# A batched matmul with scale and add: which two tiles GpSimd's queue stores, and in which groups of partitions

## The chip, the cores and the metric

One core of a Trainium2 chip. The metric is the device time of one execution in microseconds; lower is better.

## The reference

```python
batch, m, k, n = 16, 512, 1024, 768
x:         (batch, m, k) float32
weight:    (k, n)        float32
scale:     0.1
add_value: (batch, m, n) float32

def reference(x, weight, scale, add_value):
    return (scale * np.matmul(x, weight) + add_value).astype(np.float32)
```

## The kernel before

The 16 batches are taken as one matrix of 8192 rows, that is 64 tiles of 128 rows. The rows are dealt out so that partition p of a group of 16 tiles holds 16 neighbouring rows of the output: `x_v`, `add_v` and `out_v` are views with the axes partition, group, tile, column. A transfer of n tiles of one group therefore moves n x 3072 B in one piece per partition for `add_value` and `out`, and n x 4096 B for `x`.

The buffers are fixed tensors, and the kernel says by hand who waits for what. `xs` holds 16 tiles of `x` (in four "moves" of 4 tiles), `ao` holds 32 tiles: `add_value` is loaded into a slot, the result is written over it, and it is stored from there; tile t has slot t % 32, so tile t + 32 can only be loaded when tile t is stored. At the start the last slots of `ao` hold the weight.

Each engine has one job:

- SP (SyncE) issues the transfers in the order of the list `STREAM` (lines 22 to 29), all on one queue. An entry is a kind, a first tile and a number of tiles: "w" weight, "x" a load into `xs`, "a" a load of `add_value` into `ao`, "o" a store from `ao`, and "a+" a bookkeeping step with no transfer. Ahead of each entry SP waits for what it needs (`need`): an "x" for the casts that free the slots (line 116), an "a" for the earlier loads and for the stores that free its slots (lines 120 to 132), an "o" for an earlier store and for DVE's results (line 142).
- ACT (ScalarE) and GpSimd run `mover` (line 150): they cast `x` from `xs` to bfloat16 in `va`, 8 instructions each for a move, in strips of 32 partitions, laid out for the transpose.
- DVE (VectorE) casts the weight, transposes the moves into `xt` (line 178), and finishes pairs of tiles: scale times the product, plus `add_value`, into `ao` (line 187). `made` counts finished tiles.
- PE (TensorE) runs `product` (line 207): 8 weight loads and 16 matmuls per tile.

GpSimd has a second job, around which the change turns. After its first two rounds of casts (`TURN_AT = 2`, that is tiles 0 to 31) it waits until the tiles of `PAIR` are finished and stores these two tiles itself, on its own DMA queue, in three transfers that share the 128 partitions as `BY_POOL` says (lines 246 to 248). Then it goes on with its casts. SP leaves these two tiles out of its own stores, and waits for GpSimd's stores (`aside_sem`) ahead of the load that overwrites the first of the two slots:

```python
                if s <= PAIR.start + A_SLOTS <= last:
                    need(aside_sem, 16 * len(BY_POOL))
```

Before, `PAIR` is tiles 8 and 15, and the load in question is that of `add_value` for tiles 40 to 47.

Of the kernel before, what the change touches and what calls it, by code (L numbers as in the profile page):

```python
# [10 lines left out]
R = 16  # L11
X_SLOTS = 16
A_SLOTS = 32
# [8 lines left out]
STREAM = [  # L22
# [6 lines left out]
]  # L29
FIRST, ENDING = (0, 8), 48  # L30
PAIR, TURN_AT = slice(8, 16, 7), 2
BY_POOL = [(122, 6), (0, 98), (98, 24)]


@with_exitstack
def kernel(
# [23 lines left out]
    out_v = out_f.rearrange("(g p t) n -> p g t n", p=P, t=R)  # L60
# [10 lines left out]
    ao = const.tile([P, A_SLOTS, N], fp32, name="ao")  # L71
# [10 lines left out]
    aside_sem = tc.alloc_semaphore("aside")  # L82
# [8 lines left out]
        return t % A_SLOTS  # L91

    def store_pair(eng, p, n):
        assert PAIR.stop <= R and PAIR.stop <= A_SLOTS
        eng.dma_start(out_v[p:p + n, 0, PAIR, :], ao[p:p + n, PAIR, :]).then_inc(aside_sem, 16)  # L95

    def sync_engine(eng):
        groups, stores, known = 0, [], {}

        def need(sem, value):  # L100
            if known.get(sem, 0) < value:
                eng.wait_ge(sem, value)  # L102
                known[sem] = value

        for at, (op, s, n) in enumerate(STREAM):
# [14 lines left out]
            elif op == "a":  # L120
# [4 lines left out]
                if s <= PAIR.start + A_SLOTS <= last:  # L125
                    need(aside_sem, 16 * len(BY_POOL))
                if s >= A_SLOTS:
# [109 lines left out]
    s, n = FIRST  # L237
# [4 lines left out]
    with tc.tile_critical(no_gpsimd_drain=True):  # L242
        sync_engine(nc.sync)
        mover(nc.scalar, nc.scalar.copy, 0, by_act)
        mover(nc.gpsimd, nc.gpsimd.tensor_copy, 1, by_pool, pool_go, 0, TURN_AT)
        nc.gpsimd.wait_ge(made, MADE + PAIR.stop)
        for p, n in BY_POOL:
            store_pair(nc.gpsimd, p, n)
        nc.gpsimd.addr_align(HALF_BLOCK, offset=PAST, max_nops=0)
        mover(nc.gpsimd, nc.gpsimd.tensor_copy, 1, by_pool, pool_go, TURN_AT, T // X_SLOTS - TURN_AT)  # L250
        vector_engine(nc.vector)
        tensor_engine(nc.tensor)
# [40 lines left out]
```

## Time and profile before

| | |
|---|---|
| median of 3 runs | 207.06 us (207.04 to 207.12) |
| the profiled execution | 206.85 us, its span 205.5 us |
| bytes moved | 87.04 MB, of these 61.87 MB read from and 25.17 MB written to HBM |
| busy PE | 167.5 us (82%) |
| busy POOL, ACT, DVE | 137.4, 134.7, 98.0 us |
| SP's queue, GpSimd's queue | 86.25 MB, 0.79 MB |

The span runs from the first to the last instruction of the profiled execution. The queue named hardware_dynamic is SP's, the one named software_dynamic is GpSimd's. All transfers of both are carried out by the same 16 DMA engines. In the timelines a row gives start, duration, engine, line and operation, and in brackets the idle time ahead of it with what ended it.

### The profile page before, as it was taken

The page shows a single profiled execution, that of the slowest core. Times are in us where ns is not written, and L with a number is a line of the kernel's source. Part 1 is how long each engine was busy: PE and PEld are TensorE (multiplying, and loading weights), DVE is VectorE, ACT ScalarE, POOL GpSimd, SP SyncE. Part 2 cuts the span into 40 slices and gives each one's busy share as a digit, 9 for nine tenths or more (in the row PEclk, how much of TensorE's full clock was granted, in tenths as well). Part 3 has the DMA queues.
Part 4 walks back from the last instruction along what each step waited for, and adds up shares of the span by engine and source line. Part 5 has one row for each costly group of instructions (what it writes and reads, how often), then busy time and mean ns, then how long its engine had stood idle before and what let it go on. Part 6 is the DMA issues. An engine that isn't in the chain of part 4 may idle for free.

```text
span 205.5 us, 2223 instructions
## 1 busy us (share of the span) xinstructions
PE 167.5 (82%) x1008; PEld 50.4 (25%) x512; DVE 98.0 (48%) x66; ACT 134.7 (66%) x129; POOL 137.4 (67%) x135
## 2 busy tenths in 40 slices
PE   0000099999999999999999999999999997999900
PEld 0000022233322333223332233332333322333200
DVE  0004525537555555465555555555552853455330
ACT  2049980699999906999999059999991099920000
POOL 0049994699999916999999549999992099930000
PEclk9999999999999999999999999999999999999995
DMA  8989999999999899999999999999999999998997
GB/s 287 427 372 438 440 485 408 392 437 459 446 459 459 357 459 408 408 426 413 455 404 450 431 416 464 434 411 421 440 431 415 437 448 421 493 459 364 423 440 304
DMA packets 4065, 87.04 MB, mean 424 GB/s; under 512 B 480, under 2 KB 480, under 8 KB 1120
## 3 DMA queue, kind: packets, MB, share of 16 engines
q1 hardware_dynamic: 3856, 86.25, 98.1%
q0 software_dynamic: 208, 0.79, 0.9%
q14 instruction: 1, 0.01, 0.0%
HBM read 61.87 MB, written 25.17 MB: 424 GB/s over the span
## 4 chain that ended last, share of the span: by engine, by line
DMA 38%; PE 36%; POOL 10%; ACT 5%; issue 4%; DVE 3%; SPq 1%; POOLq 0%; DVEq 0%; ACTq 0%
PE mm L210 36%; DMA out_dram<-ao 22%; DMA xs<-in_x_dram 15%; POOL va L163 9%; ACT va L163 5%; DVE xt L178 2%; DVE ao L187 1%; POOL out_dram L95 1%; SPq L130 0%; SPq L118 0%; DVEq L176 0%; SPq L102 0%; POOLq L156 0%; POOLq L158 0%; POOLq L153 0%
## 5 line engine op out<-in xcount | busy, mean ns | idle before, releaser
L210 PE MATMUL mm<-w_bf,xt 128*128 128x256 bf16 (+1 forms) x1008 | 167.5, 327 | 28.0 <-DVE xt L178 27.1
L163 POOL CAST va<-xs 32x1024 bf16<-32x1024 f32 x128 | 135.2, 1056 | 44.2 <-DMA xs<-in_x_dram 36.8
L163 ACT CAST va<-xs 32x1024 bf16<-32x1024 f32 x128 | 133.4, 1042 | 45.2 <-DMA xs<-in_x_dram 42.2
L187 DVE SCALAR_TENSOR_TENSOR ao<-mm,ao 128x1536 f32 (+1 forms) x32 | 56.2, 1756 | 72.9 <-PE mm L210 68.9
L208 PEld LDWEIGHTS <-xt 128*128 128x128 bf16 x512 | 50.4, 98 | 144.6 <-issue 116.6
L178 DVE STREAM_TRANSPOSE xt<-va 128x1024 f32<-128x1024 f32 x32 | 39.4, 1234 | 8.4 <-POOL va L163 6.3
L171 DVE CAST w_bf<-ao 128x3072 bf16<-128x3072 f32 x2 | 4.5, 2240 | 18.1 <-DMA ao<-in_weight_dram 18.1
L152 ACT ACT_TABLE_LOAD x1 | 1.3, 1283 | 1.3 <-SPq L242 1.3
L95 POOL DMA_DIRECT2D out_dram<-ao x3 | 2.0, 672 | 0.0
L274 POOL MEMSET const-float32-0.0<- 128x1 f32 x1 | 0.1, 98 | 0.2 <-issue 0.2
L274 POOL MEMSET const-bfloat16-1.0<- 128x1 bf16 x1 | 0.1, 101 | 0.0
L274 POOL MEMSET const-float32-1.0<- 128x1 f32 x1 | 0.1, 98 | 0.0
L274 POOL MEMSET const-uint8-127<- 128x1 uint8 x1 | 0.1, 98 | 0.0
## 6 DMA issues: line engine op xcount, KB each, us to landing
xs<-in_x_dram SPq DMA_DIRECT2D x7, 4096.0 KB, 20.9
ao<-in_add_value_dram SPq DMA_DIRECT2D x6, 3072.0 KB, 15.7
out_dram<-ao SPq DMA_DIRECT2D x3, 3072.0 KB, 27.4
ao<-in_add_value_dram SPq DMA_DIRECT2D x1, 6144.0 KB, 24.2
out_dram<-ao SPq DMA_DIRECT2D x1, 6144.0 KB, 31.2
out_dram<-ao SPq DMA_DIRECT2D x1, 4608.0 KB, 14.9
xs<-in_x_dram SPq DMA_DIRECT2D x2, 2048.0 KB, 21.0
ao<-in_weight_dram SPq DMA_DIRECT2D x2, 1536.0 KB, 16.8
```

Of the source, the lines that this page charges most:

```text
L95: eng.dma_start(out_v[p:p + n, 0, PAIR, :], ao[p:p + n, PAIR, :]).then_inc(aside_sem, 16)
L152: eng.preload_act_table(mybir.ActivationFunctionType.Copy)
L163: copy(va[q % VA_BUFS][32 * b:32 * b + 32, :, a, :], src[32 * a:32 * a + 32, :, b, :]).then_inc(count, 1)
L171: eng.tensor_copy(w_bf[:, s:s + n, :], ao[:, W_AT + s:W_AT + s + n, :]).then_inc(casts, n)
L178: eng.transpose(xt[:, 2 * half:2 * half + 2, :, :].rearrange("p i c m -> p (i c m)"), va[move % VA_BUFS][:, q:q + 2 * KC, :, :].bitcast(fp ...
L187: eng.scalar_tensor_tensor(a, mm[:, q:q + 2, 0:N], float(scale), a, op0=mybir.AluOpType.mult, op1=mybir.AluOpType.add).then_inc(made, 2)
L208: eng.ldweights(x_j, tile_position=(0, 0))
L210: m = eng.add_instruction(mybir.InstMatmult(start_tensor_calc=(j == 0), stop_tensor_calc=(j == KJ - 1), tile_size=(P, P), tile_position=(0 ...
L274: nc = _bacc.Bacc("TRN2", target_bir_lowering=False, num_devices=1)
```

## The change

GpSimd stores tiles 16 and 23 where it stored 8 and 15. SP stores 8 to 15 whole, and 17 to 22 in place of 16 to 23. GpSimd's three transfers take 5, 48 and 75 partitions in place of 6, 98 and 24. The wait for them moves with the pair: it now stands ahead of the load of `add_value` for tiles 48 to 55. `store_pair` computes the group of the pair, since tiles 16 to 23 lie in the second group of 16.

```diff
@@ -22,14 +22,14 @@
 STREAM = [
     ("w", 0, 4), ("w", 4, 4), ("a", 0, 8),
     ("x", 8, 8), ("a", 8, 8), ("x", 16, 8), ("a", 16, 16), ("x", 24, 8),
-    ("x", 32, 8), ("a+", 16, 16), ("o", 0, 8), ("o", 9, 6), ("a", 32, 8), ("x", 40, 8),
-    ("a", 40, 8), ("x", 48, 8), ("o", 16, 8), ("o", 24, 8), ("a", 48, 8), ("x", 56, 4),
+    ("x", 32, 8), ("a+", 16, 16), ("o", 0, 8), ("o", 8, 8), ("a", 32, 8), ("x", 40, 8),
+    ("a", 40, 8), ("x", 48, 8), ("o", 17, 6), ("o", 24, 8), ("a", 48, 8), ("x", 56, 4),
     ("x", 60, 4), ("a", 56, 8), ("o", 32, 16), ("o", 48, 12),
     ("o", 60, 4),
 ]
 FIRST, ENDING = (0, 8), 48
-PAIR, TURN_AT = slice(8, 16, 7), 2
-BY_POOL = [(122, 6), (0, 98), (98, 24)]
+PAIR, TURN_AT = slice(16, 24, 7), 2
+BY_POOL = [(123, 5), (0, 48), (48, 75)]
@@ -91,8 +91,9 @@
     def store_pair(eng, p, n):
-        assert PAIR.stop <= R and PAIR.stop <= A_SLOTS
-        eng.dma_start(out_v[p:p + n, 0, PAIR, :], ao[p:p + n, PAIR, :]).then_inc(aside_sem, 16)
+        assert PAIR.start // R == (PAIR.stop - 1) // R and PAIR.stop <= A_SLOTS
+        at = slice(PAIR.start % R, (PAIR.stop - 1) % R + 1, PAIR.step)
+        eng.dma_start(out_v[p:p + n, PAIR.start // R, at, :], ao[p:p + n, PAIR, :]).then_inc(aside_sem, 16)
```

## The prediction

> **What bounds the kernel now.** I read the page first: the span, the DMA line of the 40 slices, and the queues.
>
> ```profile
> span 205.5 us, 2223 instructions
> DMA  8989999999999899999999999999999999998997
> DMA packets 4065, 87.04 MB, mean 424 GB/s; under 512 B 480, under 2 KB 480, under 8 KB 1120
> q1 hardware_dynamic: 3856, 86.25, 98.1%
> q0 software_dynamic: 208, 0.79, 0.9%
> ```
>
> The packets of SP's queue (q1) fill 98.1% of the time of 16 engines, those of GpSimd's queue (q0) 0.9%. Nothing is left to fill: 87.04 MB at 424 GB/s is the 205.3 us. No engine of arithmetic is near that; the table by stretches shows it, and that TensorE runs at the full granted clock until its work ends at 197.4.
>
> ```profile
> core 0: us, PE busy (x) PEld busy (x) DVE busy (x) ACT busy (x) POOL busy (x), PEclk, DMA share, GB/s
> 82.00:123.00 41.00, 40.79 (x250) 12.33 (x126) 22.76 (x16) 32.53 (x32) 34.20 (x36) 1.00 1.00 425
> 164.00:197.40 33.40, 30.18 (x183) 8.99 (x92) 17.23 (x12) 16.68 (x16) 16.55 (x16) 1.00 1.02 440
> 197.40:205.50 8.10, 0.00 (x0) 0.00 (x0) 0.00 (x0) 0.00 (x0) 0.00 (x0) 0.66 0.78 335
> ```
>
> PE is at 40.79 of 41 us too, but after its end come 8.1 us in which only the DMA engines work off their backlog. So the end is that of the last DMA engine, and what matters is which one that is.
>
> The views do not number the engines, but the trace's packet records give queue, size, start and duration, and a packet starts 3 or 4 ns before the previous one of its engine ends. Following this, all records fall into 16 chains, each with the same 216 data packets of q1. None has an idle time worth naming (two of 0.16 and 0.31 us). The chains, ordered by end; "6/98/24" are the packets that GpSimd's three stores put on the chain, "stores" is how much longer its store packets took than the usual one of their size:
>
> ```
> chain   6/98/24  sum  stores us  end us
> Y       1/0/2     3    0.00      204.28
> G1      1/7/0     8    0.01      204.65
> G2      1/7/0     8    0.00      204.68
> G3      1/7/0     8    0.00      204.88
> ten     0/7/2     9    0.00-0.01 204.93 to 205.42
> G4      1/7/0     8    0.20      205.37
> X       1/0/2     3    1.60      205.50
> ```
>
> This is the finding on which the forecast rests. One engine, X, is slow in every store: its 912 ns packets take 23 to 69 ns more, its 1815 ns ones 33 to 71 more, 1.60 us in all; no other has more than 0.20. X ends last although it has only 3 packets of GpSimd's, not 8 or 9. One of these packets (6144 B, two tiles of a partition) takes 0.234 us, which agrees with q0's row: 0.9% of 16 times 205.5 is 29.6 us, by 128 is 0.23. With 8, X would end at 206.67. So the split of GpSimd's stores holds X back from deciding the end, and the changed numbers are the split.
>
> **The split after.** The sets in the table show how GpSimd's queue deals partitions out: 6, 14 and 12 engines are the largest numbers up to 16 that divide 6, 98 and 24, and each transfer starts where the one before stopped: the second's 14 leave out just X and Y, the third's 12 leave out just the four G, and the first's six are these six. In ring order: four G, then X and Y (which of the two is first the trace does not say), then ten others. The Trainium skill, in DMA: Bandwidth & Descriptors, section "Why a DMA increments its semaphore by 16 and not by 1", states the same: the largest count that divides the slowest dimension, on consecutive engines from a round-robin cursor.
>
> By the same sets, 5 partitions go on 5 engines (the four G and the first of the pair), 48 on all 16 with 3 each, 75 on 15 with 5 each, starting at the second of the pair and going round to the last G. That makes 9 on each G, 4 on the first of the pair, 8 on the second and on the ten. Only one engine is relieved, not two. If X is the first: 4 for 3, X ends 0.23 later, at 205.74; G4 at 205.61, Y (+5) at 205.45, the ten 0.23 earlier. If X is the second: 8 for 3, 5 x 0.234 = 1.17 later, at 206.67.
>
> There is a third way. Before, the ring is moved on by 6 + 14 + 12 = 32, two whole turns, so every execution starts at the same engine whether or not the place is kept from one execution to the next. After it is 5 + 16 + 15 = 36: if the place is kept, each execution starts four engines on, and X has 8 or 9 packets in at least three of four. A weak sign for that: in the first load of the trace the chains start in the order X 2.247, ..., G 2.268, ..., Y 2.287, up to G 2.518, 2.627 and 2.888. Three G are the last three of 16, as if they were the last engines of the ring and X and Y close to its head; then the first transfer did not begin at the head, though it is the first of the execution.
>
> **The other edits, each at its place.** SP's order of instructions stays; two sizes change places.
>
> ```profile
> out_dram<-ao SPq DMA_DIRECT2D x1, 2304.0 KB, 28.2
> 73.13 0.82 SPq L143 DMA_DIRECT2D out_dram<-ao  x2
> 96.02 0.34 SPq L130 DMA_DIRECT2D ao<-in_add_value_dram  x1
> 96.47 0.84 SPq L118 DMA_DIRECT2D xs<-in_x_dram  x1
> ```
>
> Tiles 8 to 15 whole: 0.79 MB more in SP's queue from 73, at 424 GB/s 1.86 us per engine, ahead of add-value 32 to 39 (issued 96.02) and x 40 to 47 (96.47). Tiles 17 to 22 for 16 to 23 give the same back from 117. From there the bytes queued are as before, so add-value 48 and x 56, 60 land when they did. Sum at the end: 0. Between, x 40 lands 1.86 later, and this is what waits for it:
>
> ```profile
> 120.68 34.96 POOL L163 CAST va<-xs 32x1024 bf16<-32x1024 f32 x32 [4.95 <-DMA xs<-in_x_dram]
> 129.51 1.25 DVE L178 STREAM_TRANSPOSE xt<-va 128x1024 f32<-128x1024 f32 x1 [1.05 <-POOL va L163]
> 131.91 1.76 DVE L187 SCALAR_TENSOR_TENSOR ao<-mm,ao 128x1536 f32 x1 [1.15 <-PE mm L210]
> 174.49 1.69 PE L210 MATMUL mm<-w_bf,xt 128*128 128x512 bf16 x9 [1.13 <-DVE xt L178]
> ```
>
> GpSimd's casts start at 122.5, the transpose at 131.4, ending 132.6. PE ends tile 39 just ahead of the 131.91 row, so it stalls some 0.7 us ahead of tile 40. Before tile 56 it waits 1.13 us for data that comes no later than now: the 0.7 goes into that. Uncovered, it would push the last issue from 197.41 to 198.1, and the engines reach that store's packets only from 200.6 on (the earliest chain), X at 201.8.
>
> ```profile
> 197.41 0.33 SPq L143 DMA_DIRECT2D out_dram<-ao  x1
> ```
>
> So 0, and 0.7 as its upper bound. The wait for GpSimd's stores:
>
> ```profile
> 95.25 1.04 POOL va L163
> 96.28 1.36 POOL out_dram L95 x2
> 97.65 18.69 DMA out_dram<-ao
> ...
> 116.40 0.33 SPq L130
> 116.82 0.39 SPq L118
> 117.32 27.42 DMA out_dram<-ao
> 144.80 0.34 SPq L130 DMA_DIRECT2D ao<-in_add_value_dram  x1
> ```
>
> Now SP issues add-value 40 only when they have landed, at 116.3, with x 48 and two stores queued behind it. After, it waits for SP's store of 8 to 15: the row of 2304 KB gives about 73.5 + 28.2 + 1.86 = 103.6. So it goes out some 12.8 us sooner. That looks like much in the chain of waits (18.69 us), but the engines still work on x 40 until 118.7 at the earliest (Y) and 119.3 to 120.6 (the others): no engine idles for the lack of it. The one trace of it is that Y's first packet of add-value 40 took 0.41 us too long, on the chain with most time to spare. Worth 0 to 0.4 us, taken as 0. x 48 behind it waits for casts until 115.73 (below), so goes out half a microsecond to one sooner, onto a backlog. The wait itself moves to add-value 48, issued at 144.80, 28 us after the stores have landed: 0.
>
> ```profile
> 90.31 1.76 DVE L187 SCALAR_TENSOR_TENSOR ao<-mm,ao 128x1536 f32 x1 [1.40 <-PE mm L210]
> 78.84 17.45 POOL L163 CAST va<-xs 32x1024 bf16<-32x1024 f32 x16 [6.30 <-DMA xs<-in_x_dram]
> 96.23 2.01 POOL L95 DMA_DIRECT2D out_dram<-ao  x3
> 98.29 17.44 POOL L163 CAST va<-xs 32x1024 bf16<-32x1024 f32 x16
> ```
>
> GpSimd's own wait is now for tile 23, finished by DVE at 90.31 + 1.76 = 92.07; GpSimd gets there at 96.23. Margin 4.2 us, cost 0. If that were gone, 16 casts would be late behind it, which end at 115.73 and have 4.95 us of idle time ahead of the next. The same covers the three issues, 2.01 us for three as before, perhaps 0.1 more or less by the numbers of partitions.
>
> **Sum.** The profiled execution took 206.85 us: 1.35 around its span of 205.5; the median of the runs is 207.06, 0.21 above it. All parts but the split come to 0. X with 8 packets: 206.85 + 1.17 = 208.02, on the level of the median 208.23. That is the forecast, 208.2, or 0.6%. With 9 it is 208.46, with the timed runs' scatter 208.6; if part of the 1.60 us of X falls away, 207.9.
>
> **Rivals.** What a measurement of this kernel can tell from no change is taken as 0.2%, 0.41 us.
> First, X stays relieved: it is the first of the pair and every execution starts at the same engine. For it: X needs only one engine left out, Y has 1.2 us to spare. Against it: the 36, and that nothing in the trace puts X before Y. X has 4: 206.85 + 0.23, 207.29 at the median's level (207.0 to 207.45): no measurable change. The skill's page named above, section "Issuing engines are not separate DMA queues", also says that the queue of a transfer hardly matters, as all end on the same 16 engines; by that alone the time stays 207.06. The trace agrees that the bytes share the engines, but shows 3 to 9 packets on one engine.
> Second, faster: the wait at 116.34 costs in the timed runs, because GpSimd's stores land a little later in them and engines run dry. It decides from a landing near 118, against the 116.3 shown, and only if X stays relieved too. Price up to the 0.41 us that Y lost: 207.29 less 0.41 is 206.9, and with the ten engines' lighter load 206.6 at best.
> Third, slower through compute: x 40's 1.86 us is not absorbed, 0.7 us at the end: 207.8 with X relieved. Against it stands the slack at tile 56 and 3.2 us at the last store.
> That the stores are dealt out otherwise (48 on 12 engines, say) is possible, but X then still has 5 or fewer or 8 or more, and the two cases stand.
>
> **Chances.** Starting at the same engine each time: 0.6; X the first of the pair, given that: 0.6. This makes 0.36 for the first rival, and with the chance that the executions measured happen to be favourable 0.39. The forecast has 0.51, the second rival 0.05, the third and the like 0.05. Faster by over 0.2%: 0.05. Within 0.2%: most of the first rival and a little of the others, 0.41. Slower: 0.54. The forecast's own range is 207.9 to 208.6; to hold 8 in 10 the range must take in the first rival, so 206.95 to 208.6.
>
> **What would show it.** Chained packets after the change: one chain with 4 of GpSimd's packets, four with 9, eleven with 8; X recognisable by its long store packets. If X has 8 or 9 and ends 1.0 to 1.4 us after all others, near 206.7, the forecast is right; if X has 4, the first rival. In the views: SP issues add-value 40 near 103.6; GpSimd's casts after 115.7 wait until about 122.5; PE's wait ahead of tile 56 falls from 1.13 to some 0.4; the last store is issued at 197.4 still. Wrong would be: a last issue past 199, an idle engine between 100 and 145, or X no longer slow.

## The result, and the profile after

The changed kernel takes 208.04 us (median of 8 runs, 207.71 to 208.88), the kernel before in the same comparison 207.03 (206.97 to 207.12): ratio 1.0057, 95% interval 1.0046 to 1.0068. That is slower by 0.6%, as forecast (208.2). But the profile shows that it is slower for another reason. From the page of the changed kernel:

```profile
span 206.6 us, 2223 instructions
DMA  7989999999999999999999999999999999999996
q1 hardware_dynamic: 3856, 86.25, 97.6%
q0 software_dynamic: 192, 0.79, 0.9%
```

The bytes are the same and the span is 1.1 us longer: the time of the packets is spread over more span. Following the packets engine by engine, as the prediction did, gives this (GpSimd's packets by its three transfers; what the store packets took above the usual; the same for load packets). Where two engines end a packet within a few ns and the records allow both, the chains were laid so that X's slow packets stay together. Times of packets in this text, as in the prediction, are laid so that the last packet ends with the span; on the trace's own clock they are 0.35 to 0.51 us earlier (0.50 before, 0.38 after), which matters only where a packet is compared with an instruction.

```
changed kernel   5/48/75  sum  stores us  loads us  end us
thirteen chains           8,9  0.00       0.5-1.8   204.84 to 205.31
one G            1/3/5     9   0.27       1.2       205.77
X                1/3/0     4   1.58       1.3       205.97
last chain       0/3/5     8   0.16       2.5       206.61
```

X has 4 packets, not 8: it is the first of the pair, and it does not end last. An engine with 8 does, 1.3 us behind the thirteen. It lost most of this in single packets: 0.16 us on SP's store of tiles 8 to 15 at 102.6, 0.69 on its last load packet at 138.2, when the others had just turned to stores, 0.39 at the same turn at 175.3. None of the sixteen chains has a gap of over 0.01 us after 88 us, so no engine waits for work: this one is late by its packets alone. The timelines of SP, GpSimd and PE answer to those of before:

```profile
96.30 0.34 SPq L131 DMA_DIRECT2D ao<-in_add_value_dram  x1
96.75 0.67 SPq L119 DMA_DIRECT2D xs<-in_x_dram  x1
113.13 0.33 SPq L131 DMA_DIRECT2D ao<-in_add_value_dram  x1
115.78 0.33 SPq L119 DMA_DIRECT2D xs<-in_x_dram  x1
...
198.34 0.33 SPq L144 DMA_DIRECT2D out_dram<-ao  x1
```

```profile
96.27 1.95 POOL L96 DMA_DIRECT2D out_dram<-ao  x3
98.27 17.44 POOL L164 CAST va<-xs 32x1024 bf16<-32x1024 f32 x16
122.88 34.96 POOL L164 CAST va<-xs 32x1024 bf16<-32x1024 f32 x32 [7.17 <-DMA xs<-in_x_dram]
```

```profile
26.05 105.52 PE L211 MATMUL mm<-w_bf,xt 128*128 128x512 bf16 x630 [26.05 <-DVE xt L179]
133.01 41.77 PE L211 MATMUL mm<-w_bf,xt 128*128 128x512 bf16 x252 [1.44 <-DVE xt L179]
175.42 20.98 PE L211 MATMUL mm<-w_bf,xt 128*128 128x512 bf16 x126 [0.64 <-DVE xt L179]
```

GpSimd issues its stores at 96.27 (before: 96.23), and their first packet runs at 101.53 (before: 101.50). But before, the engines finished SP's store of 9 to 14 between 101.0 and 101.6 and were in loads when GpSimd's packets came: of its 128 packets, one starts before SP's store has ended on all engines. Now SP's store has two tiles more, ends between 103.0 and 103.8, and GpSimd's stores meet its last packets: 27 of them start before it has ended. PE waits 1.44 us ahead of tile 40 and 0.64 ahead of tile 56, and the last store is issued at 198.34, 0.9 us later than before, since x 56 to 59 land later by that much (the engine that is behind reaches them 1.07 us after the middle one). As no DMA engine ran out of work, these waits of PE and SP are not what made the time longer.

### The profile page after: what moved, and what is told of

Its sections match the earlier page's. It is cut to its first block, busy times and chain, and to the rows that moved or that the text cites. A ratio compares the mean times of both kernels' runs of the same rounds, so it can differ in the third digit from the quotient of the medians.

```text
span 206.6 us, 2223 instructions
## 1 busy us (share of the span) xinstructions
PE 167.4 (81%) x1008; PEld 50.3 (24%) x512; DVE 98.0 (47%) x66; ACT 134.7 (65%) x129; POOL 137.3 (66%) x135
## 4 chain that ended last, share of the span: by engine, by line
PE 36%; DMA 27%; POOL 18%; ACT 7%; issue 5%; DVE 3%; POOLq 0%; DVEq 0%; ACTq 0%; SPq 0%
PE mm L211 36%; DMA xs<-in_x_dram 27%; POOL va L164 17%; ACT va L164 7%; DVE xt L179 2%; POOL out_dram L96 1%; DVE ao L188 1%; POOLq L157 0%; DVEq L177 0%; ACTq L157 0%; POOLq L159 0%; POOLq L154 0%; DVEq L188 0%; POOLq L250 0%; DVEq L185 0%
```

## The experiments

Three explanations were tested in turn. Theory Y: the second engine of the pair needs its relief. Theory S: the starting place moves from one execution to the next. Theory M, formed after the first four runs: GpSimd's stores that meet SP's stores hold packets up, and an engine that is held up stays behind to the end, since its share of the bytes is fixed. The kernel before took 206.95 to 207.03 us in each of the comparisons, so the times may be set side by side.

**The pair alone, with the split of before.**

```diff
 # on the changed kernel
-BY_POOL = [(123, 5), (0, 48), (48, 75)]
+BY_POOL = [(122, 6), (0, 98), (98, 24)]
```

> The change's tiles 16 and 23, with the split of before (6, 98, 24). If the split makes the whole difference (theories Y and S below): 207.05 us, within 0.1 of before, with its small scatter; X and Y have 3 packets each. If the tiles and the shifted wait make it: near 208.0. Theory Y: the second engine of the pair, Y, is held up in loads by some 0.7 to 1.4 us in each execution, which its 5 or 6 missing packets (1.2 us) hid before. Theory S: the ring's starting place moves from one execution to the next when the engines of the three transfers do not add up to whole turns, and X is relieved only in some.

Measured 208.54 us, ratio 1.0070 (1.0056 to 1.0083). The tiles and what hangs on them make it slower by themselves, and by about as much as the whole change does (208.04, and 208.56 when it was measured again, below); that is 0.5 us above the time expected for this case. X has 3 packets and ends at 205.4; the last engine ends at 207.40. Between 101 and 106 eight packets, stores of either queue and one load beside them, took 0.18 to 1.06 us too long, 4.5 us together; before there is one, of 0.17.

**The split alone, with the tiles of before.**

```diff
 # on the kernel before
-BY_POOL = [(122, 6), (0, 98), (98, 24)]
+BY_POOL = [(123, 5), (0, 48), (48, 75)]
```

> The tiles of before (8 and 15) with the changed split (5, 48, 75). Split theories (Y and S): 208.0 us, 207.7 to 208.9, with the wide scatter of the change. Tiles and wait: 207.05. In the profile theory Y expects X with 4 packets ending near 205.7 to 206.0, and one engine of those with 8 ending last, with hold-ups of 0.3 us and more in load packets. Theory S expects X with 4 in at most one of several profiles.

Measured 207.21 us, ratio 1.0006 (0.9997 to 1.0015); the medians lie 0.11% apart. X has 4 packets and ends last, at 205.93. No packet between 101 and 106 is held up by over 0.15 us. This is the first rival of the prediction, to 0.1 us (207.29). Theories Y and S fall: Y has 8 packets here and does no harm, and all eleven runs lie between 207.00 and 207.37.

**Two attempts with four transfers** (Y loaded, X loaded):

```diff
 # on the kernel before
-BY_POOL = [(122, 6), (0, 98), (98, 24)]
+BY_POOL = [(123, 5), (0, 98), (98, 24), (122, 1)]   # e3_x_and_g
+BY_POOL = [(121, 7), (0, 98), (98, 22), (120, 1)]   # e4_not_x
```

> Tiles of before, split 5, 98, 24, 1 partitions (engines 5 + 14 + 12 + 1 = 32, two whole turns): X and its neighbour ahead, the last G, have 3 packets, Y has 9. Only the relief of Y is taken away, X keeps its 3. Theory Y: Y ends last, 206.6 to 207.0, so 208.0 to 208.4 us with wide scatter. Theory S, and theory N (the hold-ups strike any engine at random, so that the relief of Y is of no use): 207.05, since the turns are whole and X is relieved.

> Tiles of before, split 7, 98, 22, 1 partitions: Y and its neighbour behind have 3 packets, X has 8. Only the relief of X is taken away. X ends 5 x 0.234 = 1.17 us later, at 206.67, so 208.2 us, and under theory Y with small scatter, as X's 1.60 us in stores was the same in both profiles (1.58 after). If only Y matters: 207.05. The engines used are 7 + 14 + 11 + 1 = 33: under theory S the executions scatter by up to 1.2 us.

Measured 210.12 us (1.0159, 1.0138 to 1.0179) and 210.28 (1.0147, 1.0131 to 1.0163), far off every expectation. They did not test what they were made for, because the fourth transfer added something. It is not on one engine either: the trace has it as two packets of 3072 B, one for each tile, that run on two engines (in the first run both at 116.85, the trace's clock), so the engines used are 33 and 34, and not 32 and 33. Of the first run, the issue of that transfer (KB, us to landing):

```profile
out_dram<-ao POOLq DMA_DIRECT2D x1, 6.0 KB, 20.3
```

SP's timeline, and the table by stretches, whose last two columns are the DMA share and GB/s:

```profile
96.48 0.90 SPq L118 DMA_DIRECT2D xs<-in_x_dram  x1
118.75 0.33 SPq L130 DMA_DIRECT2D ao<-in_add_value_dram  x1
119.17 0.38 SPq L118 DMA_DIRECT2D xs<-in_x_dram  x1
```

```profile
112.00:117.00 5.00, 5.00 (x33) 1.46 (x16) 2.91 (x2) 1.35 (x2) 4.21 (x5) 1.00 1.02 437
117.00:122.00 5.00, 5.00 (x33) 1.49 (x16) 2.91 (x2) 1.51 (x2) 1.34 (x2) 1.00 0.90 341
122.00:127.00 5.00, 5.00 (x33) 1.55 (x16) 2.91 (x2) 4.88 (x6) 4.76 (x5) 1.00 1.02 437
```

The last transfer, 6 KB, landed only 20.3 us after its issue. With it SP issued add-value 40 at 118.75 in place of 116.40, and the engines ran dry: the DMA share falls to 0.90 and 341 GB/s between 117 and 122. The gaps of the sixteen chains there add up to 8.3 us, half a us for each on average, and single engines idle for about 2 us. This fits the second rival's threshold (a landing near 118), met from the other side: the engines run dry with the issue at 118.16 of the second run too, and do not with the 116.40 of the kernel before. The idle time is not all of the 3 us, though: in both runs nearly 30 packets between 134 and 141 are held up as well, by 20 us and more together, and why is open.

**Every engine with 8 packets.**

```diff
 # on the kernel before
-BY_POOL = [(122, 6), (0, 98), (98, 24)]
+BY_POOL = [(0, 128)]
```

> Before, with one transfer of 128 partitions in place of three: 8 packets on every engine, no engine relieved, one issue less on GpSimd. This measures alone what the forecast rested on. The forecast's price: X has 8 for 3, ends 5 x 0.234 = 1.17 us later, near 206.7 in the span, 208.2 us, and ends last. If the relief of X is of no use: 207.0.

Measured 208.07 us, ratio 1.0050 (1.0036 to 1.0063).

```profile
span 206.7 us, 2221 instructions
```

X has 8 packets, 1.55 us too many in stores, and ends last at 206.69; the fifteen others end between 204.66 and 205.38. Nothing is held up by over 0.15 us between 101 and 106. The price that the forecast put on X was right to 0.02 us of span. It is just not what the change does.

**GpSimd's stores sooner, on the kernel before, so that they meet SP's stores.** `mover` gets a parameter for which of its four moves it does.

```diff
 # on the kernel before
-        mover(..., 0, TURN_AT)
+        mover(..., 0, 1)
+        mover(..., 1, 1, (0, 1, 2))
         # wait for the pair, store it
-        mover(..., TURN_AT, T // X_SLOTS - TURN_AT)
+        mover(..., 1, 1, (3,))
+        mover(..., 2, 2)
```

> Before in tiles and split; GpSimd issues its stores one move of casts sooner (after tiles 24 to 27), so that their packets should arrive near 93 to 97, when SP's stores of 0 to 7 and 9 to 14 are under way (88 to 101), where before they arrive at 101.4, when the engines have turned to loads. Theory M (GpSimd's stores that meet SP's stores hold packets up by up to 1 us, and the engine held up stays behind to the end): several store packets between 93 and 101 take over 0.15 us too long, and the time is 207.5 to 208.5 us. Theory L (only what is late behind the tiles matters, as x 40 to 47 landing 1.86 us later): 207.0, or a little less, since the wait ahead of add-value 40 ends sooner.

Measured 209.59 us, ratio 1.0136 (1.0117 to 1.0155): slower, as theory M had it, but by 2.6 us where 0.5 to 1.5 were expected. GpSimd's packets run from 92.7 to 105.1. 9 packets are held up by over 0.15 us between 93 and 101, and 26 between 101 and 106, 13.1 us together, up to 1.31 each: the worst is where SP's store ends and the engines turn to loads. The run is not clean, though: x 40 to 47 is issued 2.3 us later here, and between 134 and 141 over 20 more packets are held up.

**GpSimd's stores later, on the changed kernel, so that they meet loads**, with the changed split and with that of before:

```diff
 # on the changed kernel (e8_late_after)
-        mover(..., 0, TURN_AT)
+        mover(..., 0, 2)
+        mover(..., 2, 1, (0,))
         # wait for the pair, store it
-        mover(..., TURN_AT, T // X_SLOTS - TURN_AT)
+        mover(..., 2, 1, (1, 2, 3))
+        mover(..., 3, 1)
 # and in e9_late_pair also
-BY_POOL = [(123, 5), (0, 48), (48, 75)]
+BY_POOL = [(122, 6), (0, 98), (98, 24)]
```

> The change, but GpSimd casts tiles 32 to 35 before it issues its stores, so that they should arrive near 110, when the engines load. Theory M: no packet held up by over 0.2 us near 102, X with 4 packets ends last near 205.9, 207.2 us as with the split alone, small scatter. Theory L: x 40 to 47 lands as late as in the change, so 208.0.

> Tiles 16 and 23 with the split of before (6, 98, 24), GpSimd's stores issued after the casts of tiles 32 to 35 as in the run before. Theory M: the 1.5 us that this pair and split cost go away, 206.9 to 207.1 us. Theory L: 208.5.

Measured 207.25 us (ratio 1.0012, 1.0003 to 1.0021; one of the eleven runs took 207.84) and 206.91 (0.9997, 0.9988 to 1.0006). Both as theory M expected; theory L falls, since x 40 to 47 lands as late as in the change. GpSimd's and PE's timelines of e8_late_after:

```profile
105.04 1.95 POOL L96 DMA_DIRECT2D out_dram<-ao  x3
107.04 8.70 POOL L164 CAST va<-xs 32x1024 bf16<-32x1024 f32 x8
122.74 35.01 POOL L164 CAST va<-xs 32x1024 bf16<-32x1024 f32 x32 [7.01 <-DMA xs<-in_x_dram]
```

```profile
26.04 169.73 PE L211 MATMUL mm<-w_bf,xt 128*128 128x512 bf16 x1008 [26.04 <-DVE xt L179]
```

The casts still wait until 122.74, but the stores now leave at 105.04, and their packets run from 109.4 on, beside loads. That PE shows no wait ahead of tile 40 has nothing to do with this: it is 1.3 us later already at its 300th matmul (78.14, in the changed kernel 76.81), before GpSimd's stores in either, and takes up tile 40 at 132.88, in the changed kernel at 133.01. X with 4 packets ends last at 205.99; with 3, in the second run, at 205.53.

**Y loaded, without a fourth transfer; and X down to 2.**

```diff
 # on e8_late_after
-BY_POOL = [(123, 5), (0, 48), (48, 75)]
+BY_POOL = [(123, 5), (0, 105), (105, 18)]   # e10_late_y: X 3, Y 9
+BY_POOL = [(123, 5), (0, 120), (120, 3)]    # e11_late_x2: X 2, Y 9
```

> Tiles 16 and 23, GpSimd's stores issued late as in e9_late_pair, split 5, 105, 18: X has 3 packets as there, but Y now has 9 in place of 3. If the relief of Y is of no use, as the two late runs suggest: 206.9 us, equal to e9_late_pair within 0.1, and Y, in step with the others, has no packet held up by over 0.3 us. If Y is an engine that is held up in loads by itself (theory Y): 207.5 to 208.5.

> The same with 5, 120, 3: X has 2 packets, Y 9, the four G 9. An attempt at a version that beats both kernels. X ends 0.23 earlier than with 3, near 205.3; the end is then that of the engine that also fetches instructions (205.57 with 8 packets, 205.77 with 9), so 206.9 to 207.1 us: no gain. If the fetch falls on an engine with 8: 206.75.

Measured 206.97 us (1.0002, 0.9993 to 1.0011) and 207.14 (1.0008, 0.9999 to 1.0017). Y with 9 packets costs nothing here, so only X needs relief. X with 2 ends at 204.99, and the last one at 205.62 is, as expected, an engine with 9 that also carried an instruction fetch (a gap of 0.30 us at 107.1 and 0.34 on the packet after it). No version beats the kernel before.

**The changed kernel once more.**

> The changed kernel unaltered, for a second profile. Theory M: X with 4 packets again, not last; two to six packets of SP's store of 8 to 15, or of GpSimd's beside them, held up by 0.15 to 1 us between 101 and 104, and one of the engines so held up ends last, 206.3 to 207.6; 208.04 us with the same scatter. Theory S (a starting place that moves): X with 8 or 9 packets, ending last.

Measured 208.56 us (207.97 to 208.85), ratio 1.0077 (1.0063 to 1.0090). X has 4 packets and ends at 205.72. Two packets of GpSimd's at 103.0 and 103.9 are held up by 0.47 and 0.53 us; the engine of the second, one with 9 packets and the instruction fetch, loses another 0.58 at the turn at 175.2 and ends last at 206.62. That is as theory M had it; but another engine, with no such packet ahead of it, also loses 0.43 at 138.1 and 0.47 at 175.9 and ends at 206.31.

The packets that took over 0.15 us too long, where GpSimd's stores come by the side of SP's store ahead of add-value 32:

```
kernel          GpSimd's packets  between 101 and 106   us, median
                run from          count  sum   longest
before          101.5             1      0.17  0.17     207.03
e2_split_only   101.6             0                     207.21
e5_even         101.6             0                     208.07 (X with 8)
after           101.5             2      0.33  0.17     208.04
e12_again       101.2             2      1.00  0.53     208.56
e1_pair_only    101.3             8      4.52  1.06     208.54
e7_early         92.7             26     13.14 1.31     209.59
e8_late_after   109.4             0                     207.25
e9_late_pair    109.3             0                     206.91
```

The first three have SP's short store, over by 101.7; after, e12_again and e1_pair_only have the long one, over between 103.7 and 104.5; e7_early has the short one and GpSimd's early packets; the last two have the long one and late packets. GpSimd's packets that start before SP's store has ended on all engines: 1 in each of the first three, 27, 29 and 33 in the next three, all 128 in e7_early, none in the last two. Of the four runs not listed, e3_x_and_g, e4_not_x, e10_late_y and e11_late_x2, none has a packet held up by over 0.15 us in this stretch.

## Why the prediction was right in its number and wrong in its reason

The number came out (208.2 for 208.04, span 206.67 for 206.6), but by luck: two errors happen to weigh about the same. X was charged with 5 packets (1.17 us) and has one more (0.23), 0.94 too much; and GpSimd's stores meeting SP's, worth 0.8, stood at nothing.

The step that failed is "All parts but the split come to 0", and in it the line on SP's stores: 1.86 us more in the queue from 73, given back from 117, "Sum at the end: 0". The bytes do cancel. What was left out is what else runs in those 1.86 us: the text had GpSimd's stores issued at 96.23 and SP's longer store still running, and did not put the two side by side. With the changed split this cost 208.04 less 207.21, 0.8 us (1.35 by the 208.56 of the second measurement); with the split of before, 208.54 less 207.0, 1.5. Moving only GpSimd's issue by one move of casts takes it back (208.04 to 207.25, 208.54 to 206.91).

The other wrong step is the choice between the ways the split could fall. X is the first of the pair and keeps 4 packets, in all four profiles with that split (after, e2_split_only, e8_late_after, e12_again). If the starting place moved on by 36 engines each time, X would be relieved in one of four, and in the timed runs of e2_split_only three of four would be near 208; all eleven are below 207.4. So the place does not move on. The weak sign taken from the order of the chains' first packets was none.

What held: the packet count by engine (9, 4 and 8), given that X is the first of the pair; that X decides where it has 8 (e5_even, 206.69 for 206.67); the first rival's price for the split, 207.29 for 207.21; that Y has time to spare; the margin of GpSimd's own wait (it issued at 96.27).

Smaller misses. Add-value 40 was to go out at 103.6 and went at 113.13: SP waits there for add-value 32 as well, an earlier need of the same entry, and the view of SP's waits between 100 and 118 has the row:

```profile
SPq L131 <- DMA ao<-in_add_value_dram: 8.9, 1, 8.9
SPq L103 <- DMA out_dram<-ao: 6.7, 1, 6.7
```

It cost nothing, as the engines had a backlog. The prediction's times of packets are 0.50 us later than the trace's own clock; so the engines work on x 40 until 118.2 and reach the last store's packets from 200.1 on, which makes two margins half a us smaller and changes no term of the sum. PE's stall ahead of tile 40 was 1.44 us for 0.7, and that ahead of tile 56 0.64 for 0.4. Of the second rival, the threshold near 118 fits the runs with four transfers, which fall over it; the kernel before stands up to 1.8 us short of it, so the change gains nothing by moving away from it.

What stays open: why packets of two queues' stores hold each other up, and why some engines lose 0.3 to 0.7 us on a packet at a turn between loads and stores and others do not. So how the 0.3 us that is held up at 102 in the changed kernel becomes the 1.1 at its end is not shown packet by packet; that the moment of GpSimd's stores decides is shown by the runs that move it alone. The engine that ends last there was 0.39 us behind the middle one at 88, ahead of any of these stores. Nor is it shown why more is held up with the split of before (4.5 us for 0.3 and 1.0). The hold-ups of all engines between 134 and 141 in the three slowest runs are not explained either.

## What to carry to other kernels

Where all DMA engines are full, the end is that of one engine, so follow the packets engine by engine, and look for one that is slow or was held up, before the chain of waits is believed. Two edits whose bytes cancel need not cancel in time: draw up which transfers run side by side in the stretch between them. And try small stores from a second queue at a moment when the first queue loads: in this kernel that took back all of the 0.8 to 1.5 us.

## What the runs showed of the hardware that was not expected

One engine took longer for its stores in all 13 profiles, by 1.4 to 1.7 us over the whole kernel, whatever the split; SP's stores show it, also while GpSimd's queue is empty. An engine that was held up did not make up for it by the end. Some lost more at the next turns between loads and stores (0.69 and 0.39 us on the last engine of the changed kernel), but not all: in the same profile an engine 0.6 us behind lost nothing there, nor did X in e5_even, 0.9 us behind at 175. From the end of GpSimd's casts to its first store packet 3.8 to 5.5 us went by on the trace's clock (105.04 to 108.84 in e8_late_after, 96.30 to 101.80 in e3_x_and_g). A transfer of 6 KB on that queue took 20.3 us to land behind three others.
